# Smaller emission steps in the two mixers: gate statistics, head outputs and query projections

## The chip, the cores and the metric

The kernel runs on one core of a Trainium2 chip. The metric is the device time of one execution in microseconds (us); the kernel before was timed three times.

## The reference

One inference step of a trunk of two layers. Each layer is FFN, mixer, FFN, each with a residual, a modulation by a conditioning vector and a layer norm. 640 tokens (512 of a sample, 128 of a prompt) of width 1024 go through the same weights; everything is fp32.

```python
def _ffn_sublayer(x, mod, j, g, b, w1, w3, w2):
    h = x * (1 + scale) + shift
    y = (jax.nn.silu(h @ w1) * (h @ w3)) @ w2
    return _layernorm(ALPHA * x + 0.5 * gate * y, g, b)
def _attend(q, k, v, mask, sink):
    s = jnp.einsum('bqhgd,bkhd->bhgqk', q, k) * (q.shape[-1] ** -0.5)
    p = jax.nn.softmax(s, axis=-1)      # sink: one more column of scores
    return jnp.einsum('bhgqk,bkhd->bqhgd', p, v)
def _rms(x, g, eps=1e-6):
    return x * lax.rsqrt(jnp.mean(x * x, -1, keepdims=True) + eps) * g
```

The mixer of the first layer ("even") joins windowed attention (8 query heads of 64, 2 key heads) with an mLSTM of 4 heads of 128, forward and backward in time. The mLSTM's input and forget gates go through log-sigmoid, cumulative sums and running maxima; these gate statistics scale every product of the heads. The mixer of the second layer ("odd") joins attention with RMS-normed queries and keys (4 x 2 heads) with an HGRN2 of 4 heads. In both, each recurrent head's output is RMS-normed, multiplied by an output gate, and projected back to width 1024 together with the attention's output.

## The kernel before

An fp32 product is done as three matmuls of high and low parts (`mm3`, L151; each matmul is L136, a transpose on TensorE is L139). Tokens lie along the free dimension in two halves of 384 and 256 (`HALVES`; three and two chunks of 128, `CHUNKS`), channels on 128 partitions. So a projection of 128 channels is 24 matmuls `pj` for each half, and one of 128 tokens into rows is 24 matmuls `pn`. Weights come by DMA as `raw` and are split on ACT (L123) and DVE (L126) into high and low parts `w`. PSUM has four pairs of banks: a1, b, a2 and m.

The whole program is static. Python code emits instructions; a scheduler puts them on the in-order engines by dependences and, where several are ready, by the order in which they were emitted. Parts of a mixer are Python generators: `weave` (L828) goes round several of them and emits one step of each, to the next `yield`. So where a generator yields sets which of its instructions stand ahead of another part's.

Three parts matter here.

- `attention` (L765) makes the queries of the first key head with `queries(0)`, then goes through ten steps of 128 queries (five tiles for each key head): scores `s`, softmax on DVE and ACT, transposes `pT`, values `pv`. After the fifth it calls `queries(1)`. Both calls are plain functions, so all their projections are emitted as one step. Even queries are made by `proj` (L554) with rope on DVE and POOL (L601); odd ones by `proj_group` (L567) with `normed` (L1168): squares, a sum by TensorE (`qss`), a power on POOL (`qrp`, L1185), its transpose (`qrt`), its spread over partitions (`qrb`) and rope.
- `mlstm_rows` (L929): the gate statistics on a tile `rows` of 64 x 640, mostly on DVE (a reciprocal L970, two cumulative sums L983 and L984, four running maxima L989 to L993), then exponentials on ACT and five transposes `pm` out of `rows`. It has one `yield`, ahead of the log-sigmoid. The rest is one step.
- `head_out` (L789), called twice at the end of each recurrent head, once for each half:

```python
ss = squares of the head's chunks, summed on ACT (junk)
rs = (ss / 128 + 1e-6) ** -0.5      # hrs, on POOL, L800
for each chunk: yn = hs * rs * gate (DVE, L133); transpose yn into ps (ho)
y = ps * g (ACT); split y into high and low
```

Heads go in pairs (0 and 1, then 2 and 3), woven with the projections `pn` of the heads to come and the output projections `po`. In the odd heads a chain of levels, matmuls `lv` between DVE and ACT updates of `harena` or `xarena`, comes ahead of the states.

Of the kernel before, what the change touches and what calls it, by code (L numbers as in the profile page):

```python
# [12 lines left out]
AF = mybir.ActivationFunctionType  # L13
ALU = mybir.AluOpType
# [3 lines left out]
P = 128  # L18
D = 1024
KD = 8  # L20
# [3 lines left out]
HALVES = ((0, 384), (384, 640))  # L24
HMAX = 384
CHUNKS = ((0, 1, 2), (3, 4))
# [23 lines left out]
class Net:  # L50
# [714 lines left out]
    def attention(self, kT, vv, queries, spec, yds, room, nsink=None):  # L765

        ar = Arena(self.xpool.tile([P, self.XN], F32R, tag="x", name="att"))
        st = ar.take(4 * NT).rearrange("p (a b) -> p a b", a=4)
        kk = ar.take(2 * 768).rearrange("p (a b) -> p a b", a=2)
        pr = self.wp.tile([P, 2, 2, 512], F32R, tag="w", name="pr")  # L770
        pr = [(pr[:, n, 0], pr[:, n, 1]) for n in range(2)]
        ks = kk[:, 0], kk[:, 1]
        qs = queries(0)
        for n in range(10):
            g, j = divmod(n, 5)
            if j == 0:
                self.att_keys(kk, kT, g)
                for b in range(2):
                    self.q_stack(st[:, 2 * b:2 * b + 2], qs[b])
            tiles, masks = spec[j]  # L780
            probs = []
            yield from self.att_probs(st[:, :, j * P:(j + 1) * P], ks, tiles, masks,
                                      None if nsink is None else nsink[:, 4 * g:4 * g + 4], room, probs)
            if n == 4:
                qs = queries(1)
            self.att_out(g, j, tiles, probs, vv, pr, yds[g])


    def head_out(self, hs, gate, g, yt, hf, scale=1.0):  # L789

        nc = self.nc
        ch = CHUNKS[hf]
        a, b = HALVES[hf]
        k = len(ch)
        ss = self.sm(4, "ss")
        for n, c in enumerate(ch):
            self.act(self.ft(P, "junk"), hs[c], AF.Square, scale=scale, accum_out=ss[:, n:n + 1])
        self.ts(ss[:, :k], ss[:, :k], 1.0 / 128.0, ALU.mult, 1e-6, ALU.add)
        rs = self.sm(4, "hrs")
        nc.gpsimd.tensor_tensor(out=rs[:, :k], in0=ss[:, :k], in1=self.mhalf[:, :k], op=ALU.pow)  # L800
        ps = self.pm("ho")
        for n, c in enumerate(ch):
            yn = self.ft(P, "yn")
            self.stt(yn, hs[c], rs[:, n:n + 1], gate[:, c], ALU.mult, ALU.mult)
            self.tr(ps[:, n * P:(n + 1) * P], yn)
        y = self.ft(b - a, "yh")
        self.act(y, ps[:, :b - a], scale=g)
        self.split(yt[0][:, a:b], yt[1][:, a:b], y)

    def out_group(self, wo, grp, acts, mod, tail=None):  # L810

# [27 lines left out]
    def even(self, mod, tail):  # L839
        nc, i = self.nc, self.i  # L840
        w, wo = i["w_in_even"][0], i["w_out_even"][0]
# [13 lines left out]
        def ev_rope(dst):  # L855
            def f(hf, p):
                n = 384 if hf == 0 else P
                self.rope(dst[hf][:, :n], p[:, :n], HALVES[hf][0], n)
                if hf == 1:
                    self.act(dst[1][:, -P:], p[:, P:2 * P])  # L860
            return f
# [23 lines left out]
        def queries(g):  # L885
            qs = [[self.ft(e - a, "q") for a, e in HALVES] for _ in range(2)]
            for n, q in enumerate(qs):
                self.proj(w, (2 * g + n) * P, ev_rope(q), "v" if g == 0 else None)
            return qs

        spec = []
# [37 lines left out]
    def mlstm_rows(self, mc, t, w):  # L929

        nc, i = self.nc, self.i
# [40 lines left out]
        self.act(u, u, AF.Ln)  # L972
        self.tt(e, e, u, ALU.mult)
        self.stt(z, z, 0.0, e, ALU.min, ALU.subtract)
        F, B = slice(0, 4), slice(32, 36)
        rmask, bc = u, d
        nc.gpsimd.memset(rmask, 1.0)
# [2 lines left out]
        for t in (bc, D0):  # L980
# [5 lines left out]
        self.tt(rt[0:64], gi, bc, ALU.subtract)  # L986
        nc.vector.tensor_copy(out=D0[F, P:NS:P], in_=bc[F, P - 1:NS - P:P])
        nc.vector.tensor_copy(out=D0[B, P - 1:NS - P:P], in_=bc[B, P:NS:P])
        scan(out=mu[F, 0:NS], data0=D0[F, 0:NS], data1=rt[F, 0:NS], initial=m0[F], op0=ALU.add, op1=ALU.max)  # L989
        scan(out=mu[F, NS:NT], data0=D0[F, NS:NT], data1=rt[F, NS:NT], initial=0.0, op0=ALU.add, op1=ALU.max)  # L990
        scan(out=mu[B, NT - 1:NS - 1:-1], data0=D0[B, NT - 1:NS - 1:-1], data1=rt[B, NT - 1:NS - 1:-1],
             initial=0.0, op0=ALU.add, op1=ALU.max)
        scan(out=mu[B, NS - 1::-1], data0=D0[B, NS - 1::-1], data1=rt[B, NS - 1::-1], initial=m0[B],  # L993
             op0=ALU.add, op1=ALU.max)

        mp = tmp.take(5)[0:64]
        nc.gpsimd.memset(mp, 0.0)
# [15 lines left out]
        for dr in range(2):  # L1013
            nc.sync.dma_start(out=self.o["new_state_b_m"][0, 0, dr].rearrange("(h o) -> h o", o=1),
                              in_=mn[32 * dr:32 * dr + 4, 4:5])

        col = mc.take(80).rearrange("p (c q) -> p c q", c=5)
        for hf, ch in enumerate(CHUNKS):
            ps = self.pm()
# [32 lines left out]
    def mlstm_head(self, h, ins, temps, yb, in_v, ma, col, tri):  # L1052

        nc, i = self.nc, self.i
        qT, kT, va, so = ins
        c5 = lambda t: t.rearrange("p (c t) -> p c t", c=5)

        kn, hs, W = c5(temps[0]), c5(kT), temps[1:3]
        qps = (temps[3], qT)

        for hf, ch in enumerate(CHUNKS):
            ps = self.pm()
# [5 lines left out]
        for hf, ch in enumerate(CHUNKS):  # L1068
            a, b = HALVES[hf]
# [19 lines left out]
        for dr in range(2):  # L1089
            r = 32 * dr + h  # L1090
            last = P - 1 if dr == 0 else 0
            for hf in range(2):
                a, b = (0, 384) if hf == 0 else (384, 512)
# [49 lines left out]
            yield  # L1143
        yb.append(self.pair("yb", in_v))
        yt = yb[-1]
        for hf in range(2):
            self.head_out([hs[:, c] for c in range(5)], so, self.v("b_norm_g", h, 1), yt, hf)


    def odd(self, mod, tail):  # L1150
        nc, i = self.nc, self.i
        w, wo = i["w_in_odd"][0], i["w_out_odd"][0]
# [15 lines left out]
        def normed(c0, dst, which, pool=None):  # L1168

            segs = (((0, 384, 0),), ((0, P, 0), (P, 2 * P, dst[1].shape[-1] - P)))  # L1170

            def ev(hf, p):
                a, b = HALVES[hf]
                ch = CHUNKS[hf]
                nch = 2 * len(ch)
                for s, e, o in segs[hf]:
                    self.act(dst[hf][:, o:o + e - s], p[:, s:e])
                sq = self.ft(b - a, "qsq")
                self.act(sq, p, AF.Square)
                pv = self.bank("a2", "qss")  # L1180
                for n in range(len(ch)):
                    self.mm(pv[:, 2 * n:2 * n + 2], sq[:, n * P:(n + 1) * P], hsel)
                rs, rp = self.sm(6, "qrs"), self.sm(6, "qrp")
                self.ts(rs[:, :nch], pv[:, 0:nch], 1e-6, ALU.add)
                nc.gpsimd.tensor_tensor(out=rp[:, :nch], in0=rs[:, :nch], in1=self.mhalf[:, 0:nch], op=ALU.pow)  # L1185

                def rest():
                    pt = self.bank("a2", "qrt")
                    for n in range(len(ch)):
                        self.tr(pt[0:2, n * P:(n + 1) * P], rp[:, 2 * n:2 * n + 2])  # L1190
                    rr = self.ft(b - a, "rr")
                    self.act(rr[0:2], pt[0:2, :b - a])
                    pb = self.bank("a2", "qrb")
                    self.mm(pb[:, :b - a], bsel, rr[0:2])
                    for s, e, o in segs[hf]:
                        d = dst[hf][:, o:o + e - s]
                        self.stt(d, d, gq[:, which:which + 1], pb[:, s:e], ALU.mult, ALU.mult)
                    n = 384 if hf == 0 else P
                    self.rope(dst[hf][:, :n], dst[hf][:, :n], a, n)
                return rest  # L1200
            return self.col_unit(w, c0, pool), ev
# [12 lines left out]
        def queries(g):  # L1214
            qs = [q0] if g == 0 else []
            new = [[self.ft(e - a, "q") for a, e in HALVES] for _ in range(len(qs), 2)]
            self.proj_group([normed(2560 + (2 - len(new) + 2 * g + n) * P, q, 0, None if g else "v") for n, q in enumerate(new)])
            return qs + new

        spec = [([0, 1, 2, 3, 4], None)] * 4 + [([5], None)]  # L1220
# [90 lines left out]
    def hgrn_head(self, h, ins, temps, yc, lmask, in_v):  # L1311

        nc, i = self.nc, self.i
        qT, ft, v, gt = ins
# [15 lines left out]
        ps = self.bank("a2", "lv")[:, :160].rearrange("p (c t) -> p c t", c=5)  # L1330
# [3 lines left out]
        for lev in range(7):  # L1334
            hh = 1 << lev
            nb = NT // (2 * hh)
            if lev < 5:
# [4 lines left out]
                ps = self.bank("a2", "lv")[:, :160].rearrange("p (c t) -> p c t", c=5)  # L1342
# [4 lines left out]
            else:  # L1347
                if lev == 5:
                    full = [self.bank(t, "full")[:, :b - a].rearrange("p (c t) -> p c t", t=P) for t, (a, b) in zip(("a2", "b"), HALVES)]
                    for hf, ch in enumerate(CHUNKS):  # L1350
                        for r in range(4):
                            c = slice(32 * r, 32 * r + 32)
# [22 lines left out]
        for d in range(2):  # L1375
            kn.append(kcs[1 - d].rearrange("p (c t) -> p c t", c=5))
            for hf, ch in enumerate(CHUNKS):
                ps = self.pm("kt")
# [4 lines left out]
        for d in range(2):  # L1383
# [6 lines left out]
            ps = self.pm("ds").rearrange("p (c t) -> p c t", c=4)  # L1390
# [9 lines left out]
        o = [self.ft(b - a, "o") for a, b in HALVES]  # L1400
        for hf, ch in enumerate(CHUNKS):
            ps = self.bank("b", "ov")
            for n, c in enumerate(ch):
                cc = slice(c * P, (c + 1) * P)
                out = ps[:, n * P:(n + 1) * P]
# [5 lines left out]
        o = [o[0][:, n * P:(n + 1) * P] for n in range(3)] + [o[1][:, n * P:(n + 1) * P] for n in range(2)]  # L1411
        yield
        yc.append(self.pair("yc", in_v))
        yt = yc[-1]

        g = self.sm(1, "hg")
        self.ts(g, self.v("c_norm_g", h, 1), 0.25, ALU.mult)
        for hf in range(2):
            self.head_out(o, gt, g, yt, hf, 0.5)


    def run(self, upto=6):
# [95 lines left out]
```

## Time and profile before

| | us |
|---|---|
| runs of the kernel before | 2823.49, 2816.35, 2825.56 |
| their median | 2823.49 |
| profiled execution, its own time | 2827.02 |
| its span | 2825.2 |
| TensorE (PE) busy | 2707.6 (96%) |
| VectorE (DVE) busy | 1774.7 (63%) |
| ScalarE (ACT) busy | 946.8 (34%) |
| GpSimd (POOL) busy | 252.6 (9%) |

The even mixer lies at about 500 to 930 us of the span, the odd one at about 1840 to 2350 us. The granted clock over the whole span is 0.978 of full speed. Busy shares are means over stages with different limits; the rows further down show the stages.

### The profile page before, as it was taken

The numbers are of one execution on the slowest core, as the hardware profiler recorded it, in microseconds if no ns is written. First come the engines' busy times: TensorE is split into PE (matmuls) and PEld (weight loads), VectorE is DVE, ScalarE is ACT, GpSimd is POOL, SyncE is SP. The second block draws the span as 40 slices with busy tenths as digits, with TensorE's granted clock in tenths as the row PEclk, the third lists the DMA queues.
The fourth block names the chain that finished last, engine by engine and source line by source line (L and its number), as shares of the span: only waits on it lengthen the run. The fifth ranks groups of instructions, "written<-read, shape, count | busy, mean of one in ns | idle before, by whom it ended". The sixth has DMA issues, their size and how long they took to land. (4 is left out here: it accounts for less than half of the span.)

```text
span 2825.2 us, 46791 instructions
## 1 busy us (share of the span) xinstructions
PE 2707.6 (96%) x19189; PEld 2590.9 (92%) x19189; DVE 1774.7 (63%) x3466; ACT 946.8 (34%) x1946; POOL 252.6 (9%) x293
## 2 busy tenths in 40 slices
PE   7999999989998999999999999999999789999998
PEld 5999999888887999999999999988788689999997
DVE  4967864686657976533796773475677678333335
ACT  3321222555544411212432122154554435213112
POOL 1000000311003100000300000041100021000003
PEclk8999999999989999999999999999999899999998
DMA  7544542221122544422264452130111224223210
GB/s 241 174 148 124 167 121 69 63 65 48 55 71 69 159 140 127 127 68 75 68 179 127 122 170 83 45 97 21 38 39 59 78 76 142 63 65 98 67 47 38
DMA packets 307187, 270.53 MB, mean 96 GB/s; under 512 B 13834, under 2 KB 257308, under 8 KB 306972
## 3 DMA queue, kind: packets, MB, share of 16 engines
q1 hardware_dynamic: 306612, 267.39, 31.9%
q8 instruction: 151, 2.47, 0.4%
q14 instruction: 64, 0.52, 0.1%
q10 hardware_dynamic: 360, 0.14, 0.0%
HBM read 258.31 MB, written 9.18 MB: 95 GB/s over the span
## 5 line engine op out<-in xcount | busy, mean ns | idle before, releaser
L136 PE MATMUL ps<-h,w 128*128 128x256 f32 (+1 forms) x7584 | 1124.8, 309 | 5.4 <-DVE h L126 2.9
L136 PEld LDWEIGHTS ps<-h,w 128*128 128x128 f32 x7584 | 1117.4, 190 | 8.5 <-DVE h L126 4.2
L136 PE MATMUL po<-g,wv 128*128 128x256 f32 (+1 forms) x4224 | 632.5, 310 | 7.9 <-DVE x L133 4.9
L136 PEld LDWEIGHTS po<-g,wv 128*128 128x128 f32 x4224 | 622.2, 189 | 14.7 <-DVE x L133 5.5
L133 DVE SCALAR_TENSOR_TENSOR x<-po,mod,x 128x128 f32<-128x128 f32 (+1 forms) x576 | 235.8, 435 | 282.1 <-PE po L136 281.3
L126 DVE TENSOR_TENSOR w<-raw,w 128x1024 fp32r<-128x1024 f32 x212 | 260.3, 1233 | 130.8 <-ACT w L123 130.3
L133 DVE SCALAR_TENSOR_TENSOR acc<-rawa,sc,acc 128x512 f32<-128x512 f32 x448 | 319.6, 757 | 11.1 <-DMA rawa<-in_ada_w 10.6
L123 ACT ACTIVATE wv<-raw 128x1024 fp32r<-128x1024 f32 x116 | 120.1, 1055 | 576.7 <-PE po L136 456.0
L123 ACT ACTIVATE w<-raw 128x1024 fp32r<-128x1024 f32 x212 | 222.8, 1056 | 161.6 <-issue 86.5
L477 POOL TENSOR_TENSOR ssq<-ssq,sq 128x384 f32<-128x384 f32 (+1 forms) x84 | 84.0, 1000 | 1722.0 <-ACT sq L123 1721.4
L123 ACT ACTIVATE g<-gt 128x384 fp32r<-128x384 f32 (+1 forms) x176 | 82.1, 466 | 400.7 <-DVE gt L126 400.6
L126 DVE TENSOR_TENSOR wv<-raw,wv 128x1024 fp32r<-128x1024 f32 x116 | 142.9, 1237 | 101.7 <-ACT wv L123 101.6
L126 DVE TENSOR_TENSOR gt<-sl,ps 128x384 f32<-128x384 f32 (+1 forms) x176 | 85.2, 484 | 181.8 <-PE ps L136 176.4
L136 PE MATMUL pj<-h,w 128*128 128x256 f32 (+1 forms) x1056 | 187.9, 319 | 0.9 <-ACT w L123 0.8
L136 PEld LDWEIGHTS pj<-h,w 128*128 128x128 f32 x1056 | 161.5, 192 | 7.1 <-issue 2.1
L123 ACT ACTIVATE sl<-ps 128x384 f32<-128x384 f32 (+1 forms) x176 | 76.1, 433 | 205.3 <-PE ps L136 205.2
L136 PE MATMUL ps<-h,wv 128*128 128x256 f32 (+1 forms) x864 | 139.9, 312 | 4.2 <-ACT h L123 1.6
L136 PE MATMUL pn<-w,h 128*128 128x256 f32 x960 | 137.7, 289 | 0.0
L136 PEld LDWEIGHTS ps<-h,wv 128*128 128x128 f32 x864 | 128.1, 189 | 8.2 <-DVE h L126 4.2
L136 PEld LDWEIGHTS pn<-w,h 128*128 128x128 f32 x960 | 125.9, 193 | 1.2
L126 DVE TENSOR_TENSOR g<-gt,g 128x384 fp32r<-128x384 f32 (+1 forms) x176 | 85.5, 486 | 28.9 <-ACT g L123 28.8
L136 PE MATMUL pj<-h,wv 128*128 128x384 f32 (+1 forms) x480 | 84.8, 326 | 2.0 <-DVE t L126 1.4
(327 smaller groups left out, 2513.9 us busy)
## 6 DMA issues: line engine op xcount, KB each, us to landing
raw<-in_ffn_w SPq DMA_DIRECT2D x264, 512.0 KB, 3.9
rawa<-in_ada_w SPq DMA_DIRECT2D x144, 512.0 KB, 3.9
raw<-in_w_in_odd SPq DMA_DIRECT2D x18, 512.0 KB
raw<-in_w_in_even SPq DMA_DIRECT2D x14, 512.0 KB, 5.4
raw<-in_w_in_even SPq DMA_DIRECT2D x16, 256.0 KB, 3.5
raw<-in_w_out_even SPq DMA_DIRECT2D x8, 512.0 KB
raw<-in_w_in_odd SPq DMA_DIRECT2D x16, 256.0 KB, 3.5
raw<-in_w_out_odd SPq DMA_DIRECT2D x8, 512.0 KB
```

Of the source, the lines that this page charges most:

```text
L123: return self.nc.scalar.activation(out=out, in_=in_, func=func, **k)
L126: return self.nc.vector.tensor_tensor(out=out, in0=in0, in1=in1, op=op)
L133: return self.nc.vector.scalar_tensor_tensor(out=out, in0=in0, scalar=s, in1=in1, op0=op0, op1=op1)
L136: return self.nc.tensor.matmul(out=out, lhsT=lhsT, rhs=rhs, start=start, stop=stop)
L477: nc.gpsimd.tensor_tensor(out=sums[1], in0=sums[1], in1=sq, op=ALU.add)
```

## The change

Three edits, all in the order of emission.

- `attention` takes its queries by `yield from`. Even queries are emitted in the steps of `proj_steps`, with their weights in the pool "v" for both calls. Odd queries are made by a loop of their own over two heads and two halves, with a `yield` after each half's matmuls; the part behind the power (`rest`) is emitted one half later.
- `head_out` becomes one generator for both halves: squares and powers of both first, then for each half a `yield`, the products `yn` (into one tile of the half's width), a `yield`, the transposes, scale and split. Each half's squares go into one junk tile.
- `mlstm_rows` yields at five more places: after the log-sigmoid, ahead of the running maxima, behind them, and twice ahead of the transposes.

```diff
@@ attention
-        qs = queries(0)
+        qs = yield from queries(0)
...
-                qs = queries(1)
+                qs = yield from queries(1)
@@ head_out
-    def head_out(self, hs, gate, g, yt, hf, scale=1.0):
+    def head_out(self, hs, gate, g, yt, scale=1.0):
...
+        rss = []
+        for ch in CHUNKS:
+            k = len(ch)
+            ss = self.sm(4, "ss")
+            junk = self.ft(P, "junk")
+            for n, c in enumerate(ch):
+                self.act(junk, hs[c], AF.Square, scale=scale, accum_out=ss[:, n:n + 1])
+            self.ts(ss[:, :k], ss[:, :k], 1.0 / 128.0, ALU.mult, 1e-6, ALU.add)
+            rs = self.sm(4, "hrs")
+            nc.gpsimd.tensor_tensor(out=rs[:, :k], in0=ss[:, :k], in1=self.mhalf[:, :k], op=ALU.pow)
+            rss.append(rs)
+        for (a, b), ch, rs in zip(HALVES, CHUNKS, rss):
+            yield
+            yn = self.ft(b - a, "yn")
+            for n, c in enumerate(ch):
+                self.stt(yn[:, n * P:(n + 1) * P], hs[c], rs[:, n:n + 1], gate[:, c], ALU.mult, ALU.mult)
+            yield
+            ps = self.pm("ho")
+            for n in range(len(ch)):
+                self.tr(ps[:, n * P:(n + 1) * P], yn[:, n * P:(n + 1) * P])
+            y = self.ft(b - a, "yh")
+            self.act(y, ps[:, :b - a], scale=g)
+            self.split(yt[0][:, a:b], yt[1][:, a:b], y)
@@ even
-                self.proj(w, (2 * g + n) * P, ev_rope(q), "v" if g == 0 else None)
+                yield from self.proj_steps(w, (2 * g + n) * P, ev_rope(q), "v")
@@ mlstm_rows
         self.stt(z, z, 0.0, e, ALU.min, ALU.subtract)
+        yield
...
         nc.vector.tensor_copy(out=D0[B, P - 1:NS - P:P], in_=bc[B, P:NS:P])
+        yield
...
+        yield
 
         mp = tmp.take(5)[0:64]
...
+        yield
+        yield
 
         col = mc.take(80).rearrange("p (c q) -> p c q", c=5)
@@ odd
-            self.proj_group([normed(2560 + (2 - len(new) + 2 * g + n) * P, q, 0, None if g else "v") for n, q in enumerate(new)])
+            late = []
+            for n, q in enumerate(new):
+                (wh, wl), ev = normed(2560 + (2 - len(new) + 2 * g + n) * P, q, 0, "v")
+                for hf, (a, b) in enumerate(HALVES):
+                    p = self.bank(("a1", "b")[hf], "pj")
+                    self.mm3(p[:, :b - a], [(wh[:, k], wl[:, k], self.hh[:, k, a:b], self.hl[:, k, a:b]) for k in range(KD)])
+                    late.append(ev(hf, p[:, :b - a]))
+                    yield
+                    if len(late) > 1:
+                        late.pop(0)()
+            late.pop(0)()
```

On TensorE at the start of the even mixer, from the last of the value transposes `vT` on (`s` scores, `pm<-ident,rows` the transposes of the gate statistics), there stands before:

```order
L136 MATMUL pj<-h,wv 128x384 x8
L136 MATMUL pj<-h,wv 128x256 x24
L136 MATMUL pj<-h,wv 128x384 x24
L136 MATMUL pj<-h,wv 128x256 x24
L136 MATMUL s_5623<-att 128x256 x2
L136 MATMUL s_5623<-att 128x128 x2
L136 MATMUL s_5632<-att 128x256 x2
L136 MATMUL s_5632<-att 128x128 x2
L139 MATMUL pm<-ident,rows 128x128 x5
```

and now:

```order
L136 MATMUL pj<-h,wv 128x256 x24
L136 MATMUL pn<-w,h 128x256 x24
L136 MATMUL pj<-h,wv 128x384 x24
L136 MATMUL pn<-w,h 128x256 x24
L136 MATMUL pj<-h,wv 128x256 x24
L136 MATMUL pn<-w,h 128x256 x24
L136 MATMUL s_5784<-att 128x256 x2
L136 MATMUL s_5784<-att 128x128 x2
L136 MATMUL s_5793<-att 128x256 x2
L136 MATMUL s_5793<-att 128x128 x2
L136 MATMUL pn<-w,h 128x256 x24
```

Blocks of 24 `pn` of the mLSTM's first head now stand between the halves of the queries: one ahead of the first of these rows and four in them. Two more score tiles follow, and then the five `pm`.

On TensorE at the end of even heads 0 and 1 (`ho` are the head outputs' transposes), before:

```order
L136 MATMUL pn<-w,h 128x256 x18
L139 MATMUL ho<-ident,yn 128x128 x2
L136 MATMUL pn<-w,h 128x256
L139 MATMUL ho<-ident,yn 128x128
L136 MATMUL pn<-w,h 128x256 x21
L139 MATMUL ho<-ident,yn 128x128
L136 MATMUL pn<-w,h 128x256
L139 MATMUL ho<-ident,yn 128x128
L136 MATMUL pn<-w,h 128x256 x20
L139 MATMUL ho<-ident,yn 128x128
```

and now:

```order
L136 MATMUL pn<-w,h 128x256 x47
L139 MATMUL ho<-ident,yn 128x128 x6
L136 MATMUL kq<-mi 128x128 x3
L136 MATMUL nmu<-ma,identr 128x384 x4
L136 MATMUL kq<-mi 128x128 x3
L136 MATMUL po<-yp,w 128x384 x2
L139 MATMUL ho<-ident,yn 128x128
```

The `pn` that stood between the halves now stand in one block ahead of the six transposes of both heads' first halves; the second halves' transposes come later, among `po`. In the odd mixer the same place has 60 `pn` and then six `ho`.

On TensorE in the odd mixer's first queries, up to the first softmax transposes `pT`, before:

```order
L136 MATMUL s_18980<-att 128x384 x2
L136 MATMUL pj<-h,wv 128x384
L136 MATMUL s_18984<-att 128x256 x2
L136 MATMUL pj<-h,wv 128x384 x2
L136 MATMUL s_18992<-att 128x384 x2
L136 MATMUL s_18996<-att 128x256 x2
L136 MATMUL pj<-h,wv 128x384 x8
L136 MATMUL s_19097<-att 128x384 x2
L136 MATMUL pj<-h,wv 128x384 x3
L136 MATMUL s_19109<-att 128x384 x2
L136 MATMUL pj<-h,wv 128x256 x14
L139 MATMUL pT<-ident,pq 128x128 x2
```

and now:

```order
L136 MATMUL pj<-h,wv 128x256 x24
L136 MATMUL s_19015<-att 128x384 x2
L136 MATMUL s_19019<-att 128x256 x2
L136 MATMUL s_19027<-att 128x384 x2
L136 MATMUL s_19031<-att 128x256 x2
L136 MATMUL s_19132<-att 128x384 x2
L136 MATMUL s_19144<-att 128x384 x2
L139 MATMUL pT<-ident,pq 128x128 x8
L136 MATMUL pv<-pr,vals 64x512 x6
```

The projections that stood between the scores and ahead of `pT` now stand earlier, between `qss` and `qrt`. Further on, at the end of the odd attention, 34 `pn` stand in one piece ahead of the first `lv`, where 120 stood.

## Rows read from the trace of the kernel before

**Rows 1.** The page, part 1: busy us of each engine, share of span, instructions.

```profile
PE 2707.6 (96%) x19189; PEld 2590.9 (92%) x19189; DVE 1774.7 (63%) x3466; ACT 946.8 (34%) x1946; POOL 252.6 (9%) x293
```

**Rows 2.** TensorE by windows: length, busy (instructions), granted clock, DMA share, GB/s.

```profile
570.00:608.00 38.00, 28.60 (x199) 0.87 0.34 93
790.00:805.00 15.00, 10.76 (x86) 1.00 0.50 63
846.00:866.00 20.00, 17.39 (x115) 1.00 0.04 8
1000.00:1050.00 50.00, 50.00 (x355) 1.00 0.43 128
1915.00:1940.00 25.00, 22.87 (x129) 0.86 0.03 9
2000.00:2046.00 46.00, 41.34 (x238) 0.96 0.12 35
2197.00:2218.00 21.00, 15.45 (x175) 1.00 0.50 155
2218.00:2246.00 28.00, 16.02 (x564) 0.51 0.09 24
2265.00:2286.00 21.00, 17.99 (x133) 1.00 0.00 1
```

**Rows 3.** Waits of TensorE, even mixer (500 to 950): total us, times, longest us.

```profile
PE pm L139 <- ACT rows L123: 8.0, 1, 8.0
PE ho L139 <- DVE yn L133: 6.9, 7, 2.6
PE pv L136 <- ACT pr L123: 4.0, 6, 2.7
```

**Rows 4.** Waits of TensorE, odd mixer (1840 to 2350).

```profile
PE lv L136 <- ACT harena L123: 8.5, 6, 2.3
PE ho L139 <- DVE yn L133: 5.7, 8, 0.8
...
PE lv L136 <- DVE harena L126: 3.6, 1, 3.6
```

**Rows 5.** Waits of TensorE, 1915 to 2046, both odd query calls.

```profile
PE qrt L139 <- POOL qrp L1185: 5.1, 6, 1.1
```

**Rows 6.** Timeline of TensorE, even start: start, us, instruction, [idle before <-releaser].

```profile
579.57 7.45 PE L136 MATMUL pj<-h,wv 128*128 128x384 f32 x48 [1.35 <-DVE t L126]
...
596.91 4.56 PE L136 MATMUL pn<-w,h 128*128 128x256 f32 x24
```

**Rows 7.** TensorE by windows where the granted clock falls.

```profile
595.00:600.00 5.00, 4.07 (x19) 0.50 0.76 209
805.00:810.00 5.00, 5.00 (x19) 0.50 1.00 342
1925.00:1930.00 5.00, 5.00 (x15) 0.50 0.00 2
2025.00:2030.00 5.00, 5.00 (x26) 0.70 0.00 0
```

**Rows 8.** Timeline of TensorE, last head output of even heads 0 and 1.

```profile
803.69 0.30 PE L139 MATMUL ho<-ident,yn 128*128 128x128 f32 x1 [2.62 <-DVE yn L133]
```

**Rows 9.** Timeline of TensorE, odd attention's first softmax.

```profile
1943.00 0.76 PE L136 MATMUL s<-att 128*128 128x384 f32 x4
...
1948.13 0.38 PE L139 MATMUL pT<-ident,pq 128*128 128x128 f32 x2
```

**Rows 10.** Timeline of TensorE, end of the odd attention.

```profile
2107.07 1.00 PE L136 MATMUL s<-att 128*128 128x128 f32 x8
...
2128.24 14.56 PE L136 MATMUL pn<-w,h 128*128 128x256 f32 x120
2142.73 0.53 PE L136 MATMUL lv<-hi,hw 128*32 128x32 f32 x38
```

**Rows 11.** Timeline of DVE, the last set-up of the first levels.

```profile
2128.44 0.83 DVE L126 TENSOR_TENSOR hw<-xarena 128x640 f32<-128x640 f32 x1
```

More of the change, by code (lines that the diff above doesn't have):

```diff
@@ L784, in attention @@
             if n == 4:
-                qs = queries(1)
+                qs = yield from queries(1)
             self.att_out(g, j, tiles, probs, vv, pr, yds[g])
-    def head_out(self, hs, gate, g, yt, hf, scale=1.0):
+    def head_out(self, hs, gate, g, yt, scale=1.0):
         nc = self.nc
[L792 to L808, printed above, removed]
+        rss = []
[21 more added lines that the diff above has]
+            self.split(yt[0][:, a:b], yt[1][:, a:b], y)
     def out_group(self, wo, grp, acts, mod, tail=None):
@@ L1145, in mlstm_head @@
         yt = yb[-1]
-        for hf in range(2):
-            self.head_out([hs[:, c] for c in range(5)], so, self.v("b_norm_g", h, 1), yt, hf)
+        yield from self.head_out([hs[:, c] for c in range(5)], so, self.v("b_norm_g", h, 1), yt)
     def odd(self, mod, tail):
@@ L1417, in hgrn_head @@
         self.ts(g, self.v("c_norm_g", h, 1), 0.25, ALU.mult)
-        for hf in range(2):
-            self.head_out(o, gt, g, yt, hf, 0.5)
+        yield from self.head_out(o, gt, g, yt, 0.5)
     def run(self, upto=6):
```

## Prediction

> **What bounds the kernel now.** First the busy table: TensorE works 2707.6 us of the 2825.2 us span [rows 1], so all its idle time is 117.6 us, and no reordering wins more than that plus what is lost at the lower clock. Next the windows of TensorE, read stage by stage. A stretch of FFN shows 50.00 busy of 50.00 [rows 2]; the edit does not touch it. The idle time lies in the mixers. The rows of [rows 2] sum it where the edit works: 9.4 us at the even mixer's start (570 to 608), 4.2 and 2.6 us at the two head outputs of the even mixer (790 to 805, 846 to 866), 2.1 and 4.7 us where the odd mixer makes queries (1915 to 1940, 2000 to 2046), 5.6, 12.0 and 3.0 us around the odd head outputs. Last the waits of TensorE, which name the releaser. Even mixer: one wait of 8.0 us of the gate transposes `pm` for `rows`, 6.9 us in seven waits of the head-output transposes `ho` for `yn`, and a longest `pv` wait of 2.7 us [rows 3]. Odd mixer: 5.7 us in eight `ho` waits and 12.1 us of the level matmuls `lv` for `harena` [rows 4], and 5.1 us in six `qrt` waits for POOL's power `qrp` in the stretch where both calls of queries run [rows 5].
>
> Some waits cost twice. After the last wait of 2.62 us for `yn` [rows 8] the granted clock is 0.50, that is 1.2 of 2.4 GHz, for 5 us; the same level stands after the gate wait (595 to 600) and in 1925 to 1930, and 0.70 on average in 2025 to 2030 [rows 7]. At half rate 5 busy us hold 2.5 us of full-rate work. A block of 24 `pn` takes 4.56 us there [rows 6] against 14.56 / 5 = 2.9 us per 24 in the long block of 120 [rows 10].
>
> **The change part by part.** No matmul, transpose or element operation is added or dropped, so engine busy time at full clock stays (the junk tile has no cost of its own). What changes is which instruction stands ahead of which. A bare `yield` issues nothing.
>
> 1. *Gate statistics.* Before, the chain reciprocal, scans, transposes is emitted nearly in one piece, all even queries stand ahead of it on TensorE, and nothing is left behind which to hide: 8.04 + 1.35 = 9.4 us idle [rows 3, 6], plus 4.07 / 2 = 2.0 us at half clock [rows 7]. Now five blocks of 24 `pn` stand among query halves and scores, 5 x 2.9 = 14.6 us of work ahead of the transposes. But the DVE chain is no shorter, and query evacuations now stand between its pieces. Ends: 11.4 us gained if all is covered, 0 if the chain is pushed back by as much. Nearest row for what remains is the 1.35 us wait of a `pj` for DVE's rope [rows 6], whose kind the alternation repeats; three of these make 4.1. I take 9.4 - 4.1 = 5.3, call it **5**, and leave the clock loss where it is.
> 2. *Even queries(1)* in steps between score steps: the `pv` wait of 2.7 us [rows 3] gets projections ahead of it. Ends 0 and 2.7, **2**.
> 3. *Even head outputs.* The square, mean, power, scale and transpose chain of both halves runs once under one block: 47 `pn` in one piece, 47 x 0.121 = 5.7 us, where the old order stops at each half. Of 6.9 us [rows 3] I leave 1.0 for heads 2 and 3, whose first transpose stands behind only 15 `po`: 5.9. The half-clock piece 805 to 810 costs 2.5 [rows 7]; I count half of it, because some short waits stay. **7.1**, ends 3 and 9.4.
> 4. *Odd queries.* Each half's `rest()` now comes one step later, so other projections lie between POOL's power and `qrt`. 5.1 us [rows 5], 0.5 left: 4.6. Clock loss there 2.5 + 0.30 x 5 = 4.0 [rows 7], half of it, 2.0. Against it: in the first call all filler is spent early, and nothing stands between the last scores and the first `pT`. Today the same spot lasts from 1943.76 to 1948.13 [rows 9], 4.4 us, of which two later score pairs still fill some 0.9; hole 3.5. Behind the waiting `pT` stand its own `pv` and then `pn`, for which nobody else waits there, so the hole costs its length and no more. Net **3.1**, ends -4.4 and 9.1.
> 5. *Odd attention's end.* Before, 120 `pn` stand ahead of the first `lv`; now 34, so 86 x 0.121 = 10.4 us of cover is gone. From the last scores (2108.1) to `lv` (2142.8) it is 34.7 us now, so about 24.3 after; DVE's last `hw` is ready at 2129.27, 21.2 us after the scores [rows 10, 11]. Just covered: **0**; below, -10.4 if attention's softmax on DVE slips.
> 6. *Odd head outputs.* 5.7 us [rows 4], 1.2 left for heads 2 and 3: **4.5**, ends 2 and 5.7. The `lv` waits on `harena` of heads 2 and 3 (16.0 busy of 28 us at a clock of 0.51 [rows 2]) are set by DVE and ACT building the next level, which the edit leaves alone: they start earlier, as late as before relative to their heads.
> 7. *Queues.* The four first weight loads on SP move ahead of stores, and the 10 small state stores move with their step. DMA is busy 0.34 of the even start and at most 0.50 in the stretches of [rows 2]: 0, ends -1 and 1.
>
> Sum 5 + 2 + 7.1 + 3.1 + 0 + 4.5 = 21.7. A new static order also has waits that the old trace cannot show; the nearest row is the longest `pv` wait, 2.7 us, and I charge one for each mixer: 21.7 - 5.4 = 16.3. The profiled execution took 2827.02 us, so 2810.7 by its own time; the three runs have a median of 2823.49, 3.5 lower, so the forecast for the median is 2823.5 - 16.3 = **2807**.
>
> On the clock: five busy us at 0.50 follow a stretch with 4.2 us idle, whose longest piece is 2.62 us [rows 8], while the stretch 846 to 866, with 2.6 us idle in all, keeps 1.00 [rows 2, 7]. The Trainium skill, "TensorE: Matmul & The Clock Gate", section "A second HAM failure mode: psum-queue depth-cycling", says that frequent tiny idles between groups of matmuls, while PSUM banks are cycled, make the clock swing between its two levels. That speaks against part 1, where TensorE now changes between `pj` and `pn` banks every 24 matmuls. The first stretch agrees with it, the second does not. By it the sum would lose another 2.5 us in part 1, and regain nothing in parts 3 and 4 (3.2 us): about 10.6 us gained. By the rows alone half comes back.
>
> **The rivals.**
> *Hidden anyway.* The transposes and powers are no longer waited for, but what stands behind them (DVE and ACT doing softmax, splits and ropes in program order) is as late as before, and TensorE waits one or two instructions further on. For: of the odd head outputs' neighbour waits, 12.1 us are on `harena`, and DVE feeds nearly every wait in [rows 3, 4]. Against: the FFN that follows is TensorE-bound. Only pieces with independent work right behind remain: the 2 of part 2 and half of the 5.9 of part 3, 5 us. Time 2818.5.
> *The clock stays up.* If the removed waits were what dropped it, parts 1, 3 and 4 get 2.0 + 1.3 + 2.0 more, and 5.4 for unseen waits is not due: 21.7 + 5.3 = 27, with the hole of part 4 also covered 30.5. Time about 2793. For: every half-clock row of [rows 7] stands right after a wait that goes. Against: the stretches at 2218 to 2246 and behind the even head outputs belong to small matmuls and stay.
> *Slower: the filler is spent too early in the odd attention.* Place: from queries(0) to the first `lv`. `pn` and `pj` that used to stand under softmax and level set-up now stand under qrt, where only 5.1 us were to be had. Price: 4.4 us of hole at the first `pT`, 10.4 us of cover lost ahead of `lv`, and a clock that falls as in 2218 to 2246, where 16.0 busy us ran at half rate (7.8 us lost): 22.6. What the even mixer gives, 14.1 less 5.4, is 8.7; so it decides from the point where holes in the odd attention exceed 8.7 us plus what the odd parts bring. If these bring nothing, 13.9 us slower: 2837. For: the margin of part 5 is only 3 us, and it rests on DVE keeping today's pace. Against: later softmax steps get as much or more filler than before.
>
> **How the numbers follow.** Forecast 0.50 (2798 to 2814 its own range), hidden anyway 0.23, clock stays up 0.13, slower 0.14. A measurement of this kernel tells 0.3%, 8.5 us, from no change: faster is below 2815, slower above 2832. Faster: 0.48 of the forecast, 0.13, and 0.05 of hidden: 0.66. Same: 0.02 + 0.18 + 0.04 of the slower case: 0.24. Slower: 0.10. The range leaves out the outer half of the clock case and most of the slower one: 2793 to 2829.
>
> **What would show it.** Right: no `pm` wait for `rows` over 3 us and over 32 us busy in the 38 us that begin as the window 570 to 608 does; `ho` waits of both mixers together under 3 us (12.6 now); `qrt` waits under 1 us in the odd attention; `lv` waits near 12 us as now. A hole at the first odd `pT` of 3 to 4 us. The hidden case shows the same waits gone and new ones of DVE or ACT of equal size within 10 us; the slower case an idle stretch of over 5 us ahead of the first `lv`. The forecast is wrong if TensorE's idle time in all does not fall by at least 8 us from 117.6, or if its time at 0.50 grows by over 10 us.

## The result and the profile after

The changed kernel took 2801.41 us (median of 4 runs, 2800.70 to 2806.68), the kernel before 2823.08 (4 runs): ratio 0.9937, 95% interval 0.9914 to 0.9960, so 18 us faster (11 to 24); the two medians lie 21.7 us apart. The forecast was 16.3 us. Timed again (e8 below), the ratio was 0.9928 (0.9913 to 0.9942). The profiled execution after took 2806.68 us, 20.3 less than that of before. Its page, part 1, as in [rows 1]:

```profile
PE 2700.8 (96%) x19189; PEld 2584.2 (92%) x19189; DVE 1771.8 (63%) x3466; ACT 945.0 (34%) x1946; POOL 249.2 (9%) x293
```

The idle time of TensorE fell by 13.5 us, from 117.6 to 104.1 (at least 8 was the forecast's condition), and its busy time by 6.8 with the same number of instructions. Its windows over the stretches of [rows 2] and of the first odd softmax, shifted to where they now lie (length, busy, granted clock, DMA share, GB/s):

```profile
568.00:606.00 38.00, 34.25 (x258) 1.00 0.29 76
780.00:795.00 15.00, 14.97 (x111) 1.00 0.36 34
829.00:849.00 20.00, 19.49 (x136) 1.00 0.05 11
...
1925.00:1940.00 15.00, 10.04 (x30) 0.63 0.00 0
...
2182.00:2197.00 15.00, 14.01 (x179) 1.00 0.70 216
2197.00:2228.00 31.00, 17.70 (x571) 0.56 0.07 22
2246.00:2266.00 20.00, 18.36 (x136) 1.00 0.00 1
```

The even start is busy for 34.25 of 38 us, at a clock of 1.00 (28.60 and 0.87 in [rows 2]). The four head outputs lost 4.2, 2.6, 5.6 and 3.0 us; now 0.0, 0.5, 1.0 and 1.6 (the third window is 6 us shorter than it was and the next one 3 us longer: together they lost 17.5 of 49 us, now 14.3 of 46). The stretch of small level matmuls is as bad as it was (17.70 of 31 us, clock 0.56). New is 1925 to 1940: 5.0 us idle, and the rest at 0.63.

The waits of TensorE, even mixer (as [rows 3]: total, times, longest):

```profile
PE pj L136 <- DVE t L126: 1.8, 1, 1.8
...
PE pj L136 <- ACT q L123: 1.0, 1, 1.0
PE pn L136 <- ACT mi L123: 0.9, 1, 0.9
...
PE ho L139 <- DVE yn L133: 0.4, 1, 0.4
```

The `pm` wait for `rows` is gone, and the long `pv` wait; three waits of 1.8, 1.0 and 0.9 us have come at the start. Odd mixer (as [rows 4]):

```profile
PE lv L136 <- ACT harena L123: 8.7, 6, 2.5
...
PE qrt L139 <- POOL qrp L1195: 3.6, 2, 2.4
PE s L136 <- ACT pq L123: 3.3, 3, 1.5
PE qss L136 <- ACT qsq L123: 3.2, 3, 1.5
PE lv L136 <- DVE harena L126: 1.9, 2, 1.5
...
PE ho L139 <- DVE yn L133: 1.9, 3, 0.9
```

The 3.6 us of `qrt` belong to the group of keys and first queries ahead of the attention, which the edit leaves alone; in the two query calls ([rows 5]: 5.1 us) there are none. Of the waits that have come, 3.1 us of `s` lie at the first softmax, behind the first call, and the 3.2 us of `qss` in the second call.

Where the time of the two profiled executions went, by events that both have: at the context transposes of the even mixer the changed kernel is 1.8 us ahead (nothing was changed there), at the end of that mixer 18.4, at the odd mixer's context transposes 16.5, at the first `lv` 14.9, at the end of the odd mixer 20.5. So the even mixer gave 16.6 us, the odd attention lost 1.5, the odd heads gave 5.6; what lies between the mixers, FFN and odd projections, lost 1.9.

For the experiments two sums are used below, both over windows of 5 us: the idle time of TensorE, and what the clock costs, its busy time times (1 - granted clock).

| stretch | | before | changed |
|---|---|---|---|
| even mixer, first `pj` to last `po` | idle / clock, us | 30.0 / 12.2 | 15.3 / 10.1 |
| odd attention, context transposes to first `lv` | idle / clock, us | 10.1 / 4.5 | 10.7 / 7.1 |
| odd heads, first `lv` to last `po` | idle / clock, us | 27.6 / 11.0 | 24.6 / 9.3 |

### The profile page after: what moved, and what is told of

The parts are those of the page before. It is cut to its first block, busy times and chain, and to the rows that moved or that the text cites. A ratio compares the mean times of both kernels' runs of the same rounds, so it can differ in the third digit from the quotient of the medians.

```text
span 2804.9 us, 46807 instructions
## 1 busy us (share of the span) xinstructions
PE 2700.8 (96%) x19189; PEld 2584.2 (92%) x19189; DVE 1771.8 (63%) x3466; ACT 945.0 (34%) x1946; POOL 249.2 (9%) x293
## 5 line engine op out<-in xcount | busy, mean ns | idle before, releaser
L133 DVE SCALAR_TENSOR_TENSOR acc<-rawa,sc,acc 128x512 f32<-128x512 f32 x448 | 319.8, 758 | 11.4 <-DMA rawa<-in_ada_w 10.7
L136 PE MATMUL pj<-h,w 128*128 128x384 f32 (+1 forms) x864 | 154.4, 319 | 0.8 <-DVE w L126 0.6
L136 PEld LDWEIGHTS pj<-h,w 128*128 128x128 f32 x864 | 132.1, 192 | 4.9 <-issue 1.3
L136 PE MATMUL pj<-h,wv 128*128 128x256 f32 (+1 forms) x672 | 112.9, 318 | 3.9 <-DVE t L126 1.8
L136 PEld LDWEIGHTS pj<-h,wv 128*128 128x128 f32 x672 | 101.4, 194 | 8.0 <-issue 2.5
```

The source lines that it names most:

```text
L133: return self.nc.vector.scalar_tensor_tensor(out=out, in0=in0, scalar=s, in1=in1, op0=op0, op1=op1)
L136: return self.nc.tensor.matmul(out=out, lhsT=lhsT, rhs=rhs, start=start, stop=stop)
```

## The experiments

All twelve were timed in five rounds against the kernel before. Ratios, with what they make of some 2825 us:

| run | ratio (95%) | us against before |
|---|---|---|
| e1 gate statistics and even queries | 0.9981 (0.9971 to 0.9992) | -5 |
| e2 head outputs | 0.9958 (0.9942 to 0.9974) | -12 |
| e3 odd queries | 1.0003 (0.9991 to 1.0016) | +1 |
| e4 all but the odd queries | 0.9917 (0.9901 to 0.9933) | -23 |
| e5 yields of the gate statistics alone | 0.9991 (0.9979 to 1.0004) | -3 |
| e6 even queries alone | 0.9974 (0.9965 to 0.9982) | -7 |
| e7 changed, first odd call as before | 0.9891 (0.9871 to 0.9911) | -31 |
| e8 the changed kernel | 0.9928 (0.9913 to 0.9942) | -20 |
| e9 as e7, no gate yields | 0.9915 (0.9900 to 0.9930) | -24 |
| e10 changed, first odd call without yields | 0.9901 (0.9882 to 0.9920) | -28 |
| e11 head outputs without yields | 0.9962 (0.9949 to 0.9975) | -11 |
| e12 e7 again | 0.9917 (0.9903 to 0.9932) | -23 |

e1 to e4, e5 to e8 and e9 to e12 shared a chip each.

**The three edits one by one.** Each of e1 to e3 has one edit of the change on the kernel before. e1 has the lines of the change in `even` and `mlstm_rows`, e2 those in `head_out` with its two calls, e3 those in `odd`. e4 is the changed kernel with

```diff
@@ odd
-            late = []
...
-            late.pop(0)()
+            self.proj_group([normed(2560 + (2 - len(new) + 2 * g + n) * P, q, 0, None if g else "v") for n, q in enumerate(new)])
```

> Only the first edit and the even queries: gate statistics in six steps, even queries in steps; head outputs and odd queries as before. Theory (each part is worth the waits that it takes away, and the parts add): the gate wait of 9.4 us becomes three waits of 3.7 us in all, the 2.0 us at half clock behind it and the pv wait of 2.7 us go: 5.7 + 2.0 + 2.5 = 10 us faster than before, ratio 0.9964. Rival (most of the even mixer's gain of some 17 us belongs to the head outputs, whose wait was followed by a low clock; the early gate statistics only move the wait): 2 to 4 us faster, ratio 0.999.

> Only the head outputs in steps, in both mixers; the rest as before. Theory (parts add): even ho waits 6.9 to under 0.5 us, odd ones 5.7 to 1.9 us, and nothing back from the clock, since the half-rate stretch of small matmuls in even heads 2 and 3 stays: 10 us faster, ratio 0.9965, and the gate wait of 8 us stays in the trace. Rival (hidden anyway: the waits go but those on harena and x grow by as much): within 3 us of before.

> Only the odd queries in steps. Theory (filler spent early: what the qrt waits give, 2 to 5 us, is lost again where scores and first pT now stand without projections, 4.9 us of waits and a half clock behind them): the odd attention takes 1.6 us longer than before; ratio 1.0005, between 0.9995 and 1.002; the trace shows the s, pT and pv waits near the first softmax. Rival (the forecast's part 4: net gain of 3.1 us): ratio 0.999.

> The changed kernel, with the odd queries as before. Theory (the odd queries' part is a small loss): 1.6 us faster than the changed kernel, so about 19 to 23 us faster than before, ratio 0.993, and the waits of s, pT and pv at the first odd softmax gone, the qrt waits back at 5 us. Rival (part 4 is a gain): 3 us slower than the changed kernel, ratio 0.995.

The product of the three ratios is 0.9942, the change itself 0.9937 and 0.9928: within the intervals the parts add. But e1 missed its own figure: 10 us were expected, 5 (2 to 8) came. In its profile the even mixer's idle time falls by 5.7 us where waits of 8.2 were to go; the `pm` and `pv` waits did go, and the largest that has come instead is one of `nmu` for `harena`, 1.9 us. The odd queries bring nothing that the times can tell: e3 cannot be told from no change, its odd attention takes 226.0 us from context transposes to first `lv` (before 224.6). e4 went as expected, but its interval overlaps that of e8 and the two did not share a chip, so e7 and e10 decide it.

In e2 the waits of the heads are gone in the even mixer, and the gate wait stays (third row, where 6.9 stood in [rows 3]):

```profile
PE pm L139 <- ACT rows L123: 8.1, 1, 8.1
...
PE num L136 <- DMA C<-in_state_b_n: 2.3, 1, 2.3
...
PE ho L139 <- DVE yn L133: 0.4, 1, 0.4
```

A wait of 2.3 us for the DMA of a state has come. The profile of the change does not show it, but that of e8, the same kernel, has 0.8 us of it, and those of e4, e7, e9, e10 and e12 have 0.6 to 1.7; the profiles with the old head outputs, and e11, have none.

**What in the first edit pays.** e5 has the five yields of `mlstm_rows` alone on the kernel before, e6 the even queries alone:

```diff
@@ even
-                self.proj(w, (2 * g + n) * P, ev_rope(q), "v" if g == 0 else None)
+                yield from self.proj_steps(w, (2 * g + n) * P, ev_rope(q), "v")
```

> Only the five yields in the gate statistics; even queries, head outputs and odd queries as before. The five pm then stand far behind, among the softmax of the first steps, and 24 pn stand between score tiles. Theory A (the yields alone carry the first edit's gain, since they keep the transposes behind other work): the pm wait of 8 us is gone, the pj wait of 1.35 us stays, 5 to 8 us faster than before. Theory B (yields and even queries in steps belong together): under 2 us.

> Only the even queries in steps, gate statistics still in one piece. The five pm then stand right behind the first 8 pj, ahead of nearly all queries and pn. Theory A and B both say slower: the chain on rows has some 12 us still to go when TensorE comes to pm, and all of it is idle, with half clock behind: pm wait of 10 to 15 us in place of 8, time 2 to 8 us longer than before. If it is not slower, the yields are not what made the gate chain harmless.

e5 decides neither theory: its 3 us (6 faster to 1 slower) reach from over 5 to under 2. The yields alone take the `pm` wait away, but the scores wait instead (waits of TensorE in e5, even mixer), and the run cannot be told from before:

```profile
PE s L136 <- ACT E L123: 3.6, 2, 3.3
PE pn L136 <- DVE t L126: 1.9, 1, 1.9
```

e6 was to be slower by both theories and is 7 us faster (5 to 10). Its timeline of TensorE has `pm` ahead of nearly all queries, as expected, and yet the wait is 5.0 us, not 10 to 15:

```profile
574.87 1.64 PE L136 MATMUL pj<-h,wv 128*128 128x384 f32 x8
581.47 1.33 PE L139 MATMUL pm<-ident,rows 128*128 128x128 f32 x5 [4.96 <-ACT rows L123]
```

The reason stands on DVE and ACT, which the gate chain shares with the attention. Before, between the copy L987 and the next piece of the chain (`rows`, 579.43) stand splits of keys and values and then rope:

```profile
576.06 0.68 DVE L987 COPY rows<-rows 4x3 f32<-4x3 f32 x1
576.13 0.60 DVE L126 TENSOR_TENSOR att<-kT,att 64x384 fp32r<-64x384 f32 x1
...
579.43 1.41 DVE L126 TENSOR_TENSOR rows<-rows 64x640 f32<-64x640 f32 x1
580.87 0.87 DVE L988 COPY rows<-rows 4x3 f32<-4x3 f32 x1
```

In e6 the chain runs through:

```profile
574.91 0.68 DVE L987 COPY rows<-rows 4x3 f32<-4x3 f32 x1
574.99 0.80 DVE L126 TENSOR_TENSOR rows<-rows 64x640 f32<-64x640 f32 x1
575.82 0.16 DVE L988 COPY rows<-rows 4x3 f32<-4x3 f32 x1
```

From the start of the reciprocal to `pm` it is 29.8 us before (566.16 to 595.93) and 16.5 in e6 (565.01 to 581.47). Of the 13.3 us between them some 10 lie on DVE: 2.4 us of key and value splits, 4.9 of rope and splits of queries and 1.1 of a weight's split stand between the chain's pieces, and some pieces took longer than in e6 (1.41 against 0.80 us for the `rows` shown; why, no run shows). The other 3.2 lie on ACT, where a split of queries and the load of an activation table stand ahead of the last exponential that `pm` reads. This is that exponential before (timeline of ACT):

```profile
595.14 0.73 ACT L123 ACTIVATE rows<-rows 64x640 f32<-64x640 f32 x1
```

The changed kernel lies between the two. Its reciprocal (timeline of DVE) and the same exponential (ACT):

```profile
562.84 4.14 DVE L976 RECIPROCAL rows<-rows 64x640 f32<-64x640 f32 x1
583.87 0.74 ACT L123 ACTIVATE rows<-rows 64x640 f32<-64x640 f32 x1
```

From the start of the one to the end of the other it is 21.8 us, against 29.7 before, and `pm` follows only at 603.99. So the gate wait was long in good part because work of the attention, emitted ahead, stood inside the chain. What stands ahead of `pm` on TensorE counts as well: e6, which puts it early, still waits 5.0 us there.

**The hole in the odd attention.** e7 is the changed kernel with the old code for the first call of the odd queries:

```diff
@@ odd
+            if g == 0:
+                self.proj_group([normed(2560 + (2 - len(new) + 2 * g + n) * P, q, 0, None if g else "v") for n, q in enumerate(new)])
+            else:
...
```

e10 keeps the new loop and drops its yields in the first call (only the second call, g = 1, keeps them):

```diff
                     late.append(ev(hf, p[:, :b - a]))
-                    yield
+                    if g:
+                        yield
```

> The changed kernel with the first call of the odd queries as before and the second in steps. Theory (the loss of the odd queries is the hole at the first softmax, which comes from the first call; the second call takes qrt waits away and costs nothing): 2 to 5 us faster than the changed kernel, and at least as fast as the version with all odd queries as before. Rival (the second call's waits move to qss and s, no gain): equal to the version with all odd queries as before, within 1 us in the odd attention's length.

> The changed kernel itself beside the others on one chip: ratio to the kernel before 0.992 to 0.996 as already seen; the differences to the others are read against it.

> The changed kernel, with the new loop of the odd queries and its late rest, but without the yields in the first call. Theory (the hole at the first odd softmax comes from the yields alone, which let projection steps be emitted beside the two query halves that then lack under the softmax): no hole, odd attention as long as with the first call as before (217.7 us from the context transposes to the first lv, against 226.0 of the changed kernel), 6 to 10 us faster than the changed kernel. Rival (the late rest of the first call makes it, by putting qrt and rope later): hole stays, same time as the changed kernel.

On one chip e7 took 2796.50 us (2793.51 to 2799.54), the changed kernel 2807.06 (2805.16 to 2808.14): 10.6 us faster, more than expected. In the profiles the odd attention takes 217.7 us in e7, 219.1 in e12 (the same kernel) and 215.2 in e10, against 226.1 and 226.0 in the two profiles of the changed kernel and 223.6 to 224.6 in the seven runs with both calls as before (224.5 in e4). So the second call in steps takes 5 to 7 us off the attention (e4 to e7 and e12), and the first one adds 7 to 8, net of the `qrt` waits that it takes away. The times of the whole kernel do not resolve what the second call is worth: e4 and e12, on different chips, are both 23 us under before. This is the hole, in the timeline of TensorE after:

```profile
1919.81 5.11 PE L136 MATMUL pj<-h,wv 128*128 128x384 f32 x36
1926.46 1.98 PE L136 MATMUL s<-att 128*128 128x384 f32 x8 [1.55 <-ACT pq L123]
1929.96 2.03 PE L136 MATMUL s<-att 128*128 128x384 f32 x4 [1.53 <-ACT pq L123]
1933.38 2.46 PE L139 MATMUL pT<-ident,pq 128*128 128x128 f32 x8 [1.39 <-DVE pq L130]
1936.32 3.12 PE L136 MATMUL pv<-pr,vals 128*64 128x512 f32 x6 [0.47 <-ACT pr L123]
```

Four waits, 4.9 us, and then the clock: from 1925 to 1940, 10.04 busy us at 0.63 are 6.3 us of full-rate work in 15 us, 8.7 lost. The same 15 us in e7 lose 1.0:

```profile
1925.00:1940.00 15.00, 13.96 (x93) 1.00 0.19 55
```

e10 has late `rest` parts but no yields and no hole: the yields make it. The reading that fits is that two of the projections' steps are emitted beside the two query halves and are then missing under the softmax: in e10 `pj` stand between the scores and ahead of `pT` again.

**What in the other edits can be left out.** e9 is e7 without the five gate yields; e11 is the kernel before with the new body of the head output and none of its yields; e12 is e7 again.

> The version with only the second odd call in steps, but without the five yields in the gate statistics. Theory (the gate chain was late because query evacuations stood between its pieces on DVE and ACT; even queries in steps let it run through, and the yields add nothing): within 2 us of the version with them; one pm wait of 4 to 6 us in place of three waits of 3.7 us. Rival (the yields carry it): 5 us or more slower.

> The kernel before, with the new body of the head output (squares and powers of both halves first, one wide tile yn) but none of its four yields. Theory (what pays is that other heads' and projections' steps come between power, products and transposes, which the yields do): ho waits stay over 6 us in both mixers together, 0 to 5 us faster than before, against 12 us for the whole head edit. Rival (doing both halves' squares and powers at once is enough): 10 us or more faster.

> The version with only the second odd call in steps again, beside the three others: ratio to before 0.989 as seen (0.987 to 0.991).

e9 and e12 took 2799.70 and 2799.68 us: the yields in the gate statistics add nothing that the times can tell once the even queries go in steps. As expected, e9 has one `pm` wait of 5.0 us in place of short ones (two of together 2.5 us in e12). e12 itself missed its range: 0.987 to 0.991 was expected and 0.9917 came, so the gain of this kernel over before was 31 us on one chip and 23 on the other. e11 is a miss too. The `ho` waits stay over 6 us, as expected (7.7 in all, 12.6 before; here the even mixer, with 4.0 us more in the odd one):

```profile
PE pm L139 <- ACT rows L123: 8.0, 1, 8.0
...
PE ho L139 <- DVE yn L133: 2.7, 3, 0.9
...
PE ho L139 <- DVE ss L130: 1.0, 1, 1.0
```

but it is 11 us faster (7 to 14), as the rival says. The profiles are 14.0 us apart. Of this, 5.9 us are idle time that is gone (even mixer 30.0 to 25.4, odd heads 27.6 to 26.3), against 8.7 us in e2 (24.8 and 24.1). The rest is a higher clock in e11's profile, 7.8 us over the even mixer, the odd projections and the odd heads. How much of that belongs to the edit is open, because the clock's cost differs as much between executions of the same instructions (last section). So the new body (squares and powers of both halves first, one wide `yn`, one junk tile; which of them counts was not tried apart) gives most of the head edit; the yields' 3 us of idle time are not resolved by the times.

e7, e9, e10 and e12 all beat the kernel before: 0.989 to 0.992. Against the changed kernel only e7 was timed on one chip, 10.6 us under it; the intervals of e9, e10 and e12, taken on another chip, overlap that of e8.

## Why the prediction was right, step by step

The time was 18 us (11 to 24) under before, forecast 16.3, and the likeliest case was the right one. Two steps of its mechanism were not (terms 1 and 3), and the sum came out in part by luck (term 5). Its terms:

1. *Gate statistics (5) and even queries(1) (2).* Forecast 7; e1 measured 5 (2 to 8). Right in size within that interval, and the waits that remain are almost those that were counted, 3.7 us against three of 1.35:

```profile
573.38 3.02 PE L136 MATMUL pn<-w,h 128*128 128x256 f32 x24
578.23 3.14 PE L136 MATMUL pj<-h,wv 128*128 128x256 f32 x24 [1.82 <-DVE t L126]
582.26 3.13 PE L136 MATMUL pn<-w,h 128*128 128x256 f32 x24 [0.89 <-ACT mi L123]
586.43 4.43 PE L136 MATMUL pj<-h,wv 128*128 128x384 f32 x24 [1.03 <-ACT q L123]
...
603.99 0.73 PE L139 MATMUL pm<-ident,rows 128*128 128x128 f32 x5
```

The clock, which the sum left low here, is 1.00 in 568 to 606. The mechanism was half wrong: cover by `pn` (work that TensorE does while others are waited for) was taken to be what pays, with a chain "no shorter" and evacuations (the work that takes results out of PSUM) only now between its pieces. They stood there before; the chain became 8 us shorter in the changed kernel and 13 in e6, and `pm` comes 19.4 us after it has ended (584.61 to 603.99), so by this profile the five blocks were more cover than was needed. The yields that the term was named after add nothing that the times can tell (e9). The rule that the prediction weighed, the Trainium skill, "TensorE: Matmul & The Clock Gate", section "A second HAM failure mode: psum-queue depth-cycling", does not show here: TensorE changes between `pj` and `pn` banks with three short waits, and the clock stays at 1.00.

2. *Head outputs (7.1 even, 4.5 odd).* Forecast 11.6; e2 measured 12 (7 to 16). The `ho` waits fell from 12.6 to 2.3 us in the changed kernel (1.0 and 1.2 were to be left: 0.4 and 1.9 are). The 1.3 us of clock counted with the even ones are not shown: in the changed kernel no such wait is left in 780 to 795 (14.97 of 15 us busy), and the clock falls a little later all the same, to 0.50 in 810 to 815, behind 1.7 us of idle time in short pieces in 800 to 805. So that low clock did not hang on the long `ho` wait alone.

3. *Odd queries (3.1).* This term failed: 1 us slower (3 faster to 5 slower) in e3. The gain side was not too high: 6.6 forecast for both calls, and the second alone takes 5 to 7 us off the odd attention in the profiles. The hole was mis-sized: 3.5 was set, idle time alone. It is 8.7 us in that window (1.0 in e7), 5.0 of them idle and the rest clock. The forecast counted the clock where waits go and not where one comes.

4. *Odd attention's end (0).* Right. The first `lv` follows its 34 `pn` without a wait, 22.5 us after the last scores (2105.3):

```profile
2104.16 1.11 PE L136 MATMUL s<-att 128*128 128x128 f32 x8
...
2123.64 4.23 PE L136 MATMUL pn<-w,h 128*128 128x256 f32 x34
2127.80 0.53 PE L136 MATMUL lv<-hi,hw 128*32 128x32 f32 x38
```

5. *A wait of 2.7 us for each mixer that the old trace cannot show (-5.4).* One came in the odd mixer, the `qss` waits of the second call (3.2 us; 0.6 us of `qss` waits before); the `s` waits beside them are the hole of term 3. In the even mixer nothing of that size did, and it gave 16.6 us in the profile where 11.4 were forecast. Here lies the luck: without this charge the sum was 21.7, and the single edits measured 5 + 12 - 1 = 16, each to within 3 to 5 us. The 5.7 us between them are 2 of the first term and 4 of the third, losses in places that the forecast had priced, and the charge for places that it could not see happened to cover them.

The rivals: hidden anyway fails on e2, where the waits of the heads go and 12 us with them. The slower case had its place right (the first odd `pT`) and the lower clock behind it, but the cover ahead of `lv` held. The case of a clock that stays up is not what happened: the changed kernel's clock cost in the table falls by 1.2 us in all, and the runs that reach its time (e7, 2796.5) do so by undoing a hole.

## What to carry to other kernels

When a generator is cut into smaller steps, look at what is emitted beside each new step: every round also spends one step of the other parts, which then lacks as cover further on. A long wait for a chain on another engine can be a chain that others have cut into, and then taking their instructions out of it shortens the chain itself. A new wait on TensorE can bring a lower clock behind it, and that belongs in its price: the hole's four waits of 4.9 us did, the three waits of 3.7 us at the even start did not.

## What the runs showed of the hardware

The granted clock falls at different places in executions of the same instructions. Up to the end of the even mixer, e3 has the order of before on TensorE, row for row but for one pair that has changed places. Before, in the heads 2 and 3 (TensorE by window):

```profile
821.00:836.00 15.00, 14.76 (x53) 0.54 0.11 37
```

e3, the same place:

```profile
821.00:836.00 15.00, 14.69 (x108) 1.00 0.12 39
```

Nearly equal busy time, twice the matmuls. That is 14.76 x 0.46 = 6.8 us in one stretch, and over the even mixer 12.2 against 7.4 us of clock cost. The odd projections ahead of the context transposes, which stand in one order in before, the changed kernel (twice), e2 and e3, cost 4.2, 4.3, 6.2, 8.0 and 6.1 us of clock there. So one profile of each kernel does not tell a change of the clock by less than some 5 us for a mixer; the hole's does stand out, since the clock's cost in the odd attention is 7.1 us in all three runs that have it and 0.0 to 4.5 in the others.
